# The delta-rule chain in full 128x128 matmuls, and three scale-and-bias products moved to ScalarE

## The chip, the cores and the metric

The kernel runs on one core of one Trainium2 chip. The metric is device time in microseconds of one execution. A core has five engines with a queue each, worked off in order: TensorE (PE in the profile), VectorE (DVE), ScalarE (ACT), GpSimd (POOL), and SyncE (SP), which issues the DMAs here. [...] TensorE writes PSUM; its weights are loaded by a separate instruction, shown as PEld.

## The reference

One decoder block on 512 rows of width 1024: an RMSNorm, a token mixer with two parallel branches (HGRN2 and RWKV-7) merged by sigmoid gates, and a gated convolutional FFN. The change touches both branches of the mixer. The RWKV-7 branch is this recurrence, for 16 heads of width 64:

```
def step(state, inp):                       # _rwkv7_scan
    r_t, w_t, k_t, v_t, a_t, b_t = inp
    sa = einsum('bhvk,bhk->bhv', state, a_t)
    state = state * w_t + sa[..., None] * b_t + v_t[..., None] * k_t
    y = einsum('bhvk,bhk->bhv', state, r_t)
    return state, y
```

The HGRN2 branch needs, per channel, `f = lb + (1 - lb) * sigmoid(hf)` and `k = 1 - f`, running products of `f` within half-chunks of 16 rows, and from these chunked attention scores. The RWKV key is `kr * (1 + (a - 1) * k_a)` with a constant `k_a` per channel.

## The kernel before

The program has two parts. The first, from about 55 us on, is the token mixer: for each of 66 blocks of 128 output columns a product of x with the input weights (`gemm`, L1144: 24 matmuls into the PSUM tile `zps`, or `vps` for the HGRN values; the operands are split into a high and a low fp32r half, so three matmuls for each of 8 pieces of the contraction), and beside it the two branches, for `hb` = 0 to 7 (128 channels, that is two RWKV heads). The second part, from about 743 us on, is the branch outputs, the mix and the FFN; nothing in it changes.

In the first part the order on every engine is not written out: generators (`front`, `solve`, `chain`, `hgrn`, `load`, `splits`, `evac`, `gemm`) yield operations, and `Plan` (L78 to L241) keeps a model time for each engine and issues the operation that can start first, with a rank and a bonus. `Plan.cost` holds the model's durations. The issue itself is L207, so that nearly all instructions of this part stand under that line; they are told apart by tiles.

For each `hb`, `front` (L702) makes from r, k, v and the decays the scaled operands of 8 chunks of 64 rows: `gt` (queries), `lr` (two masked 64x64 score blocks per chunk and head), `bkn` (keys, transposed). All three lie in one tile `X`. `solve` (L817) inverts the triangular blocks: `Q`. Then `chain` (L872) runs the 8 chunks one after the other; each is a step of the recurrence, with `h` the head, 0 or 1, on its own half of the partitions:

- z: `gt` times `sv` (state of one head above, values below), 128x64 weights, one matmul per head into halves of the tile `us`;
- y, first part: the same with the query columns of `gt`, into `yp`;
- `zs` is z copied out of PSUM by VectorE;
- u: `Q` times `zs`, 64x64 weights, one matmul per head;
- VectorE scales u by `rn2` into `sv`, one instruction per head;
- s: `bkn` times `sv`, 128x64 weights, one per head (not in the last chunk);
- y, second part: `lr` times `sv`, 64x64 weights, one per head, added to `yp` in PSUM;
- VectorE adds s to `sp`, the decayed state that ScalarE has made, for the next chunk's `sv`.

All these operands are fp32, and an fp32 matmul has two records in the profile (so x4 there is two matmuls). That makes 10 matmuls a step, in five pairs of which each covers half of TensorE's columns, or a quarter of its array, at a time. Behind the last step `chain` normalises y and stores it. `front` of `hb` waits for `chain` of `hb` - 2, whose `X` it takes; `chain` waits for `solve`; the `gemm` blocks fill the rest.

In `hgrn` (L966) VectorE makes the two halves of `f2` from `hf` by a scale and a bias (L972 to L975) and scans them into `p2`; GpSimd makes `hk` (L984), and in `front` the key factor `k2` (L736).

Of the kernel before, what the change touches and what calls it, by code (L numbers as in the profile page):

```python
# [16 lines left out]
P = 128  # L17
# [60 lines left out]
class Plan:  # L78
# [73 lines left out]
    def cost(self, op):  # L152
# [92 lines left out]
def block_kernel(ctx: ExitStack, tc: tile.TileContext, out: bass.AP, xT: bass.AP, xN: bass.AP,  # L245
# [146 lines left out]
    sgx = [pers.tile([P, NCH, 65], F32, name=f"sgx{i}") for i in range(2)]  # L392
# [3 lines left out]
    f2 = pers.tile([P, 2, 16, 17], F32, name="f2")  # L396
# [4 lines left out]
    for t_ in sgx:  # L401
        Gi.memset(t_[:, :, 0:1], 0.0)
    Gi.memset(f2[:, :, :, 0:1], 0.0)
# [256 lines left out]

    zwah = pers.tile([P, S], F32R, name="zwah")
# [40 lines left out]
    def front(hb):  # L702
# [13 lines left out]
        sg = sgx[hb % 2]  # L716
# [19 lines left out]
        yield G1.tensor_scalar(k2, ta, hka[:, hb : hb + 1], oka[:, hb : hb + 1], op0=ALU.mult, op1=ALU.add)  # L736
# [16 lines left out]
        lr = X[:, 4 * S : 6 * S].rearrange("p (n x c) -> p n x c", n=NCH, x=2)  # L753
        bkn = X[:, 6 * S : 8 * S].rearrange("p (n c) -> p n c", n=NCH)
# [17 lines left out]
        for h in range(2):  # L772
            q, o = hs[h], hs[1 - h]
            for half in range(2):
# [6 lines left out]
                yield V1.tensor_tensor(lr[q, n0 : n0 + 4, h], sc[q, :, h], mr[q, n0 : n0 + 4], op=ALU.mult)  # L781
                yield V1.tensor_tensor(lr[q, n0 : n0 + 4, 1 - h], sc[q, :, 1 - h],
# [10 lines left out]
        for h in range(2):  # L793
            for b in range(4):
                p0 = 64 * h + 16 * b
                yield D1.dma_start(lb_d[:, h, b].rearrange("n s t -> s n t"),
                                   lr[p0 : p0 + 16, :, h, 16 * b : 16 * b + 16])
        st_[hb] = [vt[hb], gt, lr, bkn, pel, rn2]
        fin.add(("lb", hb))
        plan.spawn("solve", solve(hb, lb_d, lr))  # L800
# [9 lines left out]
        for half in range(2):  # L810
            tp = pf.tile([P, 4, P], F32, name="tp", tag="f")
            for n in range(4):
                yield T1.transpose(tp[:, n], bks[:, 4 * half + n], ident)
            yield A1.copy(bkn[:, 4 * half : 4 * half + 4], tp)
        fin.add(("front", hb))

    def solve(hb, lb_d, lr):  # L817
# [16 lines left out]
        Q = mx.tile([P, NCH, 64], F32, name="Q", bufs=2)  # L834
# [5 lines left out]
        for n in range(NCH):  # L840
            for h in range(2):
                yield T1.matmul(fps[hs[h], n], lr[hs[h], n, h], Tn[hs[h], n], start=True, stop=True)
        fm = mx.tile([P, NCH, 64], F32, name="fm")
# [5 lines left out]
        yield V1.tensor_tensor(Q, Q, dps, op=ALU.add)  # L849
        yield V1.transpose(Tn.rearrange("p n c -> p (n c)"), Q.rearrange("p n c -> p (n c)"))  # L850
        fps2 = pf.tile([P, NCH, 32], F32, name="fps2", tag="s", bufs=1)
        fm2 = fm[:, :, 0:32]
        for h in range(2):
            a, b = slice(64 * h, 64 * h + 32), slice(64 * h + 32, 64 * h + 64)
            for n in range(NCH):
                yield T1.matmul(fps2[b, n], lr[a, n, h, 32:64], Tn[a, n, 0:32], start=True, stop=True)
# [8 lines left out]
        for h in range(2):  # L865
            a = slice(64 * h, 64 * h + 32)
            yield A1.copy(Q[a, :, 32:64], dps2[a])
        yield done(("front", hb))
        st_[hb].append(Q)
        fin.add(("solve", hb))  # L870

    def chain(hb):  # L872
        v, gt, lr, bkn, pel, rn2, bo, Q = st_.pop(hb)
        sv = mx.tile([P, NCH, 2, 64], F32, name="sv")
        vp = pus.tile([P, NT, P], F32, name="vp", tag="us")
# [48 lines left out]
        ys = mx.tile([P, NCH, 64], F32, name="ys")  # L924
        ym = small.tile([P, NCH], F32, name="ym")
        yield V1.tensor_reduce(ym, yp, axis=AX.X, op=ALU.add)
        yield V1.tensor_single_scalar(ym, ym, 1.0 / 64, op=ALU.mult)
        yield V1.tensor_tensor(ys, yp, ym.unsqueeze(2).broadcast_to([P, NCH, 64]), op=ALU.subtract)
        yield A1.activation(yp, ys, AF.Square)
        yss = small.tile([P, NCH], F32, name="yss")  # L930
        yield V1.tensor_reduce(yss, yp, axis=AX.X, op=ALU.add)
# [34 lines left out]
    def hgrn(hb):  # L966
        hf = hf_[hb]

        def c32(ap):
            return ap.rearrange("p (n c) -> p n c", n=16)  # L970

        yield V1.tensor_scalar(f2[:, 0, :, 1:17], c32(hf)[:, :, 15::-1], fb[:, hb : hb + 1], fa[:, hb : hb + 1],  # L972
                               op0=ALU.mult, op1=ALU.add)
        yield V1.tensor_scalar(f2[:, 1, :, 1:17], c32(hf)[:, :, 16:32], fb[:, hb : hb + 1], fa[:, hb : hb + 1],
                               op0=ALU.mult, op1=ALU.add)  # L975
        p2 = mx.tile([P, 2, 16, 17], F32, name="p2")
        yield V1.tensor_tensor_scan(p2.rearrange("p a n c -> p (a n c)"), f2.rearrange("p a n c -> p (a n c)"),
# [6 lines left out]
        yield G1.tensor_scalar(hk, hf, nfb[:, hb : hb + 1], fb[:, hb : hb + 1], op0=ALU.mult, op1=ALU.add)  # L984
# [57 lines left out]
        qs = mx.tile([P, 16, 32], F32, name="qs")  # L1042
        yield V1.tensor_tensor(qs, qi[:, 0:16], cq.rearrange("p t j -> p (t j)").unsqueeze(2).broadcast_to([P, 16, 32]),
# [473 lines left out]
```

## Time and profile before

| | us |
|---|---|
| time, median of 3 runs | 1256.02 (1255.92 to 1258.85) |
| profiled execution | 1255.5 |
| its span, first to last instruction | 1253.8 |
| busy in the span: PE, DVE, ACT, POOL | 1210.6, 732.7, 463.6, 536.0 |
| the second part's first matmul (`yps`) | 743.5 |

A start in the timeline is when an instruction begins; matmuls are pipelined, so the distance from one start to the next is what a matmul costs TensorE, and the duration beside it, which runs over the next ones, is not. The profile writes the weights' size of a matmul as 128\*64 (rows times columns), behind it the shape that it writes.

### The profile page before, as it was taken

The numbers are of one execution on the slowest core, as the hardware profiler recorded it, in microseconds if no ns is written. First come the engines' busy times: TensorE is split into PE (matmuls) and PEld (weight loads), VectorE is DVE, ScalarE is ACT, GpSimd is POOL, SyncE is SP. The second block draws the span as 40 slices with busy tenths as digits, with TensorE's granted clock in tenths as the row PEclk, the third lists the DMA queues.
The fourth block names the chain that finished last, engine by engine and source line by source line (L and its number), as shares of the span: only waits on it lengthen the run. The fifth ranks groups of instructions, "written<-read, shape, count | busy, mean of one in ns | idle before, by whom it ended". The sixth has DMA issues, their size and how long they took to land.

```text
span 1253.8 us, 19765 instructions
## 1 busy us (share of the span) xinstructions
PE 1210.6 (97%) x7748; PEld 949.7 (76%) x7748; DVE 732.7 (58%) x1563; ACT 463.6 (37%) x825; POOL 536.0 (43%) x420
## 2 busy tenths in 40 slices
PE   8889999999999999999999999999999999999997
PEld 6667668667668677686767888888988888888886
DVE  6988887787888988886746304335523232322213
ACT  5533334333343443343332532225534343342321
POOL 6444224342332423242424454432466575565631
PEclk9889899999999999999999999999999999999999
DMA  5121212112112122121221733254323232232332
GB/s 178 50 68 58 65 43 87 49 55 68 50 61 64 54 65 68 43 75 55 70 72 49 240 118 118 86 186 156 130 85 115 90 112 84 84 101 80 122 101 84
DMA packets 54061, 111.01 MB, mean 89 GB/s; under 512 B 21584, under 2 KB 24784, under 8 KB 53968
## 3 DMA queue, kind: packets, MB, share of 16 engines
q1 hardware_dynamic: 53968, 109.75, 27.6%
q8 instruction: 61, 1.00, 0.3%
q14 instruction: 32, 0.26, 0.1%
HBM read 100.29 MB, written 9.44 MB: 88 GB/s over the span
## 4 chain that ended last, share of the span: by engine, by line
PE 75%; DVE 15%; issue 3%; ACT 3%; POOL 2%; DMA 1%; SPq 0%; DVEq 0%; POOLq 0%; ACTq 0%
PE zps L207 20%; PE zps L323 6%; PE zps L322 6%; PE zps L321 6%; PE dn L321 3%; PE dn L323 3%; PE dn L322 3%; PE us L207 3%; PE sc L207 2%; PE yps L321 2%; PE yps L323 2%; PE yps L322 2%; PE vps L207 2%; PE mix L207 2%; DVE X L207 2%
## 5 line engine op out<-in xcount | busy, mean ns | idle before, releaser
L207 POOL TENSOR_TENSOR wlo_t<-raw,whi_t 128x512 fp32r<-128x512 f32 x134 | 184.6, 1397 | 351.3 <-ACT whi_t L207 319.8
L279 POOL TENSOR_TENSOR wlo_t<-raw,whi_t 128x1024 fp32r<-128x1024 f32 x80 | 194.6, 2439 | 96.4 <-ACT whi_t L279 96.2
L207 PE MATMUL zps<-xl,whi_t 128*128 128x512 f32 x488 | 201.3, 413 | 0.0
L207 PE MATMUL zps<-xh,wlo_t 128*128 128x512 f32 x488 | 201.2, 412 | 0.0
L207 PE MATMUL zps<-xh,whi_t 128*128 128x512 f32 x488 | 200.6, 411 | 0.0
L279 ACT CAST whi_t<-raw 128x1024 fp32r<-128x1024 f32 x80 | 83.3, 1049 | 175.5 <-DMA raw<-wup 64.5
L1378 DVE SCALAR_TENSOR_TENSOR u<-zps,pr,u 128x511 f32<-128x511 f32 x40 | 30.0, 750 | 190.7 <-ACT u L1377 190.7
L207 ACT CAST whi_t<-raw 128x1024 fp32r<-128x1024 f32 x71 | 74.4, 1048 | 147.1 <-PE zps L207 68.1
L321 PE MATMUL zps<-x2h,whi_t 128*128 128x512 f32 x320 | 125.5, 392 | 0.0
L323 PE MATMUL zps<-x2h,wlo_t 128*128 128x512 f32 x320 | 125.5, 392 | 0.0
L322 PE MATMUL zps<-x2l,whi_t 128*128 128x512 f32 x320 | 125.5, 392 | 0.0
L207 PEld LDWEIGHTS zps<-xl,whi_t 128*128 128x128 f32 x488 | 92.5, 190 | 20.6 <-issue 0.5
L207 PEld LDWEIGHTS zps<-xh,wlo_t 128*128 128x128 f32 x488 | 92.7, 190 | 20.1 <-issue 0.2
L207 PEld LDWEIGHTS zps<-xh,whi_t 128*128 128x128 f32 x488 | 92.8, 190 | 19.4 <-issue 0.2
L321 PEld LDWEIGHTS zps<-x2h,whi_t 128*128 128x128 f32 x320 | 60.2, 188 | 13.5
L322 PEld LDWEIGHTS zps<-x2l,whi_t 128*128 128x128 f32 x320 | 60.2, 188 | 13.5
L323 PEld LDWEIGHTS zps<-x2h,wlo_t 128*128 128x128 f32 x320 | 60.1, 188 | 13.4
L1403 POOL TENSOR_TENSOR th<-th,u 128x512 f32<-128x512 f32 x22 | 28.4, 1292 | 71.2 <-DVE u L1379 71.2
L207 ACT ACTIVATE sp<-sv,pel 64x64 f32<-64x64 f32 x96 | 33.0, 344 | 67.0 <-DVE sv L207 65.8
L207 PEld LDWEIGHTS us<-sv,X 128*64 128x64 f32 (+1 forms) x480 | 23.8, 134 | 39.7 <-issue 11.6
L207 DVE TENSOR_SCALAR sv<-us,rn 64x64 f32<-64x64 f32 x128 | 35.8, 280 | 29.0 <-PE us L207 25.3
L321 PE MATMUL yps<-oh,whi_t 128*128 128x512 f32 x128 | 50.2, 392 | 0.0
(375 smaller groups left out, 2601.0 us busy)
## 6 DMA issues: line engine op xcount, KB each, us to landing
raw<-win SPq DMA_DIRECT2D x64, 512.0 KB, 3.7
raw<-wup SPq DMA_DIRECT2D x44, 512.0 KB, 3.5
raw<-wdn SPq DMA_DIRECT2D x22, 512.0 KB, 3.5
raw<-wbr SPq DMA_DIRECT2D x16, 512.0 KB, 3.4
raw<-whi SPq DMA_DIRECT2D x8, 512.0 KB, 3.5
raw<-wout SPq DMA_DIRECT2D x8, 512.0 KB, 3.5
xt<-xT SPq DMA_DIRECT2D x8, 256.0 KB, 6.4
oa_d<-hg SPq DMA_DIRECT2D x8, 256.0 KB, 2.2
```

What stands on the lines that cost most here:

```text
L207: op.ins_ = self.seq(op.key, op.fn(*op.args, **op.kw))
L279: return A.copy(hi, raw), eng.tensor_tensor(lo, raw, hi.bitcast(F32), op=ALU.subtract)
L321: T.matmul(o, lh, rh, start=start, stop=False)
L322: T.matmul(o, lh, rl, start=False, stop=False)
L323: T.matmul(o, ll, rh, start=False, stop=stop)
L1378: V.scalar_tensor_tensor(u[:, 1:S], ps[:, 0 : S - 1], pc("cw1", b), u[:, 1:S], op0=ALU.mult, op1=ALU.add)
L1403: G.tensor_tensor(th, th, uv_, op=ALU.mult)
```

## The change

In `chain`, each pair becomes one or two matmuls over the whole array. z and the first part of y are one matmul per head, with all 128 columns of `gt`. `Q` is put into `qd`, a 128x128 block-diagonal tile per chunk (zeros elsewhere, set once by GpSimd for its two buffers), so u is one matmul for both heads. `lr` and `bkn` become `w2`, 128x128 per chunk and head, so s and the second part of y are one matmul per head; the block of `lr` that only `solve` needs is overwritten with zeros at the end of `solve`. Five matmuls a step stand where ten did, each with 128x128 weights and a moving operand of 64 columns, also in the first and last step.

The two parts of y now come out of different matmuls, and ScalarE copies them, per step and head, into `ys` and `yb`; VectorE adds these once per `hb`. The copy of z and the scaling of u are divided: VectorE takes head 0, ScalarE head 1. The results of a step take five of 16 slots in two PSUM banks. `f2` is gone: ScalarE writes `p2`, and the scan works in place; `hk` and `k2` also go to ScalarE. `sgx`, `Q`, `fm`, `qs` lose a buffer or share one. `Plan.cost` gets one more line.

```
+            elif n == 64 and m == 128:
+                op.us = 0.112
...
-        yield G1.tensor_scalar(k2, ta, hka[:, hb : hb + 1], oka[:, hb : hb + 1], op0=ALU.mult, op1=ALU.add)
+        yield A1.activation(k2, ta, AF.Identity, scale=hka[:, hb : hb + 1], bias=oka[:, hb : hb + 1])
...
-        lr = X[:, 4 * S : 6 * S].rearrange("p (n x c) -> p n x c", n=NCH, x=2)
-        bkn = X[:, 6 * S : 8 * S].rearrange("p (n c) -> p n c", n=NCH)
+        w2 = X[:, 4 * S : 8 * S].rearrange("p (n h c) -> p n h c", n=NCH, h=2)
...
+        qd = qds[hb % 2]
+        if hb < 2:
+            yield G1.memset(qd, 0.0)
...
+        for h in range(2):
+            yield A1.copy(qd[hs[h], :, hs[h]], Q[hs[h]])
...
+        for h in range(2):
+            yield G1.memset(w2[hs[h], :, 1 - h, hs[h]], 0.0)
         yield done(("front", hb))
...
+        for h in range(2):
+            yield G1.memset(sv[hs[h], 0, h], 0.0)
...
         for n in range(NCH):
-            for h in (1, 0):
-                yield T1.matmul(us[hs[h], zslot], gt[kp, n, h, h], sv[kp, n, h], start=True, stop=True)
-            for h in (1, 0):
-                yield T1.matmul(yp[hs[1 - h], n], gt[kp, n, h, 1 - h], sv[kp, n, h], start=True, stop=False,
-                                skip_group_check=True)
+            for h in range(2):
+                yield T1.matmul(zy[h], gt[:, n, h].rearrange("p x c -> p (x c)"), sv[:, n, h], start=True, stop=True)
             zs = small.tile([P, 64], F32, name="zs")
-            yield V1.tensor_copy(zs, us[:, zslot])
+            yield V1.tensor_copy(zs[hs[0]], zy[0][hs[0]])
+            yield A1.copy(zs[hs[1]], zy[1][hs[1]])
...
-            for h in (1, 0):
-                yield T1.matmul(us[hs[h], uslot], Q[hs[h], n], zs[hs[h]], start=True, stop=True)
             for h in range(2):
-                q = hs[h]
-                yield V1.tensor_scalar(sv[q, n, h], us[q, uslot], rn2[q, n : n + 1], None, op0=ALU.mult)
-            if n < NCH - 1:
-                for h in (1, 0):
-                    yield T1.matmul(us[hs[h], sslot], bkn[:, n, hs[h]], sv[:, n, h], start=True, stop=True)
-            for h in (1, 0):
-                yield T1.matmul(yp[hs[1 - h], n], lr[hs[h], n, 1 - h], sv[hs[h], n, h], start=False, stop=True,
-                                skip_group_check=True)
+                yield A1.copy(ys[hs[1 - h], n], zy[h][hs[1 - h]])
+            yield T1.matmul(us, qd[:, n], zs, start=True, stop=True)
+            yield V1.tensor_scalar(sv[hs[0], n, 0], us[hs[0]], rn2[hs[0], n : n + 1], None, op0=ALU.mult)
+            yield A1.activation(sv[hs[1], n, 1], us[hs[1]], AF.Identity, scale=rn2[hs[1], n : n + 1])
+            for h in range(2):
+                yield T1.matmul(sy[h], w2[:, n, h], sv[:, n, h], start=True, stop=True)
...
+            for h in range(2):
+                yield A1.copy(yb[hs[1 - h], n], sy[h][hs[1 - h]])
...
+        yield V1.tensor_tensor(ys, ys, yb, op=ALU.add)
...
-        yield V1.tensor_scalar(f2[:, 0, :, 1:17], c32(hf)[:, :, 15::-1], fb[:, hb : hb + 1], fa[:, hb : hb + 1],
-                               op0=ALU.mult, op1=ALU.add)
+        yield A1.activation(p2[:, 0, :, 1:17], c32(hf)[:, :, 15::-1], AF.Identity, scale=fb[:, hb : hb + 1],
+                            bias=fa[:, hb : hb + 1])
...
-        yield G1.tensor_scalar(hk, hf, nfb[:, hb : hb + 1], fb[:, hb : hb + 1], op0=ALU.mult, op1=ALU.add)
+        yield A1.activation(hk, hf, AF.Identity, scale=nfb[:, hb : hb + 1], bias=fb[:, hb : hb + 1])
```

What stands in a row on TensorE, before, in the fourth step of `hb` = 1 (the first `us` row and the `yp` row are z and the first part of y, the last row is u; shapes are those written, `X` holds `gt`, `lr` and `bkn`, and `bps` belongs to the bonus term):

```order
L207 MATMUL bps<-rkh,blk1r 128x512
L207 MATMUL bps<-rkl,blk1r 128x512
L207 MATMUL us<-sv,X_1205 64x64 x2
L207 MATMUL yp<-sv,X_1205 64x64 x2
L207 MATMUL zps<-xh,whi_t 128x512
L207 MATMUL zps<-xl,whi_t 128x512
L207 MATMUL zps<-xh,wlo_t 128x512
...
L207 MATMUL us<-zs,Q 64x64 x2
```

And in the changed kernel, in a step of `hb` = 1 (first u, then, past `aps` of the next block and four `zps`, s with the second part of y, one matmul per head, in slots of the tiles `us` and `yp`):

```order
L209 MATMUL us<-zs,qd_517 128x64
L209 MATMUL aps<-zwah,lw 128x512
L209 MATMUL aps<-zas,lw 128x512
L209 MATMUL zps<-xh,wlo_t 128x512
L209 MATMUL zps<-xh,whi_t 128x512
L209 MATMUL zps<-xl,whi_t 128x512
...
L209 MATMUL us<-sv,X_1203 128x64
L209 MATMUL yp<-sv,X_1203 128x64
```

What moved: no row of the chain is 64x64 on either axis of the array any more, and each stands singly or in twos between the wide rows. Counted along the whole of the first part on TensorE, a row that uses part of the array follows one that uses all of it in 240 places before and in 114 now; the number of runs of the other part-array matmuls (`sc`, `hsc`, `fps`, `dps`) is 110 before and 107 now.

On ScalarE, before, in a step of `hb` = 2, the chain has only the two decayed states `sp` (the other rows are the split of the next weights, an evacuation of `zps`, and the copy of transposed keys):

```order
L207 CAST whi_t<-raw 128x1024
L207 ACTIVATE r<-zps,cm 128x512
L207 ACTIVATE sp<-sv,pel 64x64 x2
L207 COPY X_2628<-tp 128x512
```

In the changed kernel, a whole step of `hb` = 2 on ScalarE:

```order
L209 COPY zs<-yp 64x64
L209 ACTIVATE sp<-sv,pel 64x64 x2
L209 COPY ys<-yp 64x64 x2
L209 CAST whi_t<-raw 128x1024
L209 ACTIVATE sv<-yp,rn_1804 64x64
L209 ACTIVATE hq<-zps 128x512
L209 ACTIVATE sgx<-wps,hw_128 128x8x64
L209 COPY yb<-yp 64x64 x2
```

What moved: half of z's copy and half of u's scaling now stand in this queue, with the states, the y copies and, here, a weight split between them.

More of the change, by code (lines that the diff above doesn't have):

```diff
@@ L391, in block_kernel @@
     Gi.memset(mh, 1.0)
-    sgx = [pers.tile([P, NCH, 65], F32, name=f"sgx{i}") for i in range(2)]
+    sgx = pers.tile([P, NCH, 65], F32, name="sgx")
     m65 = pers.tile([P, NCH, 65], F32, name="m65")
@@ L400, in block_kernel @@
     scm = pers.tile([P, NT, P], F32, name="scm")
-    for t_ in sgx:
-        Gi.memset(t_[:, :, 0:1], 0.0)
-    Gi.memset(f2[:, :, :, 0:1], 0.0)
+    Gi.memset(sgx[:, :, 0:1], 0.0)
     Gi.memset(scm, 0.0)
@@ L659, in c8 @@
         return ap.rearrange("p (n c) -> p n c", n=NCH)
+    qds = [mx.tile([P, NCH, P], F32, name=f"qd{i}") for i in range(2)]
     zwah = pers.tile([P, S], F32R, name="zwah")
@@ L715, in front @@
         yield T1.matmul(wps, lw[:, 0:P], zws, start=False, stop=True)
[L716 removed]
+        sg = sgx
         yield A1.activation(sg[:, :, 1:65], c8(wps), AF.Tanh, scale=0.5, bias=hw0[:, hb : hb + 1])
@@ L796, in front @@
                 yield D1.dma_start(lb_d[:, h, b].rearrange("n s t -> s n t"),
-                                   lr[p0 : p0 + 16, :, h, 16 * b : 16 * b + 16])
-        st_[hb] = [vt[hb], gt, lr, bkn, pel, rn2]
+                                   w2[p0 : p0 + 16, :, 1 - h, p0 : p0 + 16])
+        st_[hb] = [vt[hb], gt, w2, pel, rn2]
         fin.add(("lb", hb))
-        plan.spawn("solve", solve(hb, lb_d, lr))
+        plan.spawn("solve", solve(hb, lb_d, w2))
         bks = bk.rearrange("p n x c -> p n (x c)")
@@ L813, in front, with solve @@
                 yield T1.transpose(tp[:, n], bks[:, 4 * half + n], ident)
-            yield A1.copy(bkn[:, 4 * half : 4 * half + 4], tp)
+            dst = w2[:, 4 * half : 4 * half + 4].rearrange("p n h c -> p n (h c)")
+            dst = bass.AP(dst.tensor, dst.offset, [list(dst.ap[0]), [2 * P, 4], [P + 64, 2], [1, 64]])
+            yield A1.copy(dst, tp.rearrange("p n (h c) -> p n h c", h=2))
         fin.add(("front", hb))
-    def solve(hb, lb_d, lr):
+    def solve(hb, lb_d, w2):
         if hb > 0:
@@ L841, in solve @@
             for h in range(2):
-                yield T1.matmul(fps[hs[h], n], lr[hs[h], n, h], Tn[hs[h], n], start=True, stop=True)
-        fm = mx.tile([P, NCH, 64], F32, name="fm")
+                yield T1.matmul(fps[hs[h], n], w2[hs[h], n, 1 - h, hs[h]], Tn[hs[h], n], start=True, stop=True)
+        fm = Tn
         yield V1.tensor_tensor(fm, fps, mf.unsqueeze(1).broadcast_to([P, NCH, 64]), op=ALU.mult)
@@ L855, in solve @@
             for n in range(NCH):
-                yield T1.matmul(fps2[b, n], lr[a, n, h, 32:64], Tn[a, n, 0:32], start=True, stop=True)
+                yield T1.matmul(fps2[b, n], w2[a, n, 1 - h, b], Tn[a, n, 0:32], start=True, stop=True)
         for h in range(2):
@@ L923, in chain @@
         yield D1.dma_start(lgr, wlg[hb, :, 2 * P : 3 * P])
[L924 removed]
+        yield V1.tensor_tensor(ys, ys, yb, op=ALU.add)
         ym = small.tile([P, NCH], F32, name="ym")
[L926 removed]
+        yield V1.tensor_reduce(ym, ys, axis=AX.X, op=ALU.add)
         yield V1.tensor_single_scalar(ym, ym, 1.0 / 64, op=ALU.mult)
[L928 to L929 removed]
+        yield V1.tensor_tensor(ys, ys, ym.unsqueeze(2).broadcast_to([P, NCH, 64]), op=ALU.subtract)
+        yield A1.activation(yb, ys, AF.Square)
         yss = small.tile([P, NCH], F32, name="yss")
[L931 removed]
+        yield V1.tensor_reduce(yss, yb, axis=AX.X, op=ALU.add)
         yield from rsq1(yss, NCH, 64 * GN_EPS)
```

40 lines of the change are left out of this document (21 added, 19 removed).

## Prediction

> **What bounds the kernel now.** I read the page first: what each engine was busy for, and the chain of work that ended last.
>
> ```profile
> PE 1210.6 (97%) x7748; PEld 949.7 (76%) x7748; DVE 732.7 (58%) x1563; ACT 463.6 (37%) x825; POOL 536.0 (43%) x420
> PE 75%; DVE 15%; issue 3%; ACT 3%; POOL 2%; DMA 1%; SPq 0%; DVEq 0%; POOLq 0%; ACTq 0%
> ```
>
> TensorE carries three quarters of that chain. The change lies in the first part, so I cut that out by windows, and asked in its steady stretch, 140 to 620 us, what TensorE's matmuls waited for (waiter, releaser: us in total, times, longest).
>
> ```profile
> 55.00:700.00 645.00, 619.18 (x5060) 464.08 (x5060) 511.05 (x1278) 239.11 (x514) 224.83 (x198) 0.98 0.21 63
> PE us L207 <- DVE sv L207: 3.9, 6, 1.8
> ...
> PE sc L207 <- DVE sv L207: 0.2, 1, 0.2
> L207 ACT ACTIVATE sgGB<-zps x8: 585/588/592, 706.3 to 746.1; 128x512 f32<-128x512 f32 x8
> ```
>
> The eight rows of waits, of which these are the first and the last, add up to 14.4 us in 480: 3%. VectorE (third number of the window, 511 of 645) is the next engine, ScalarE (239) has room. The last row is the evacuation of the last eight weight blocks: these run on TensorE until 746 us, while the chain's last scaling (its row is below) is at 681. So the first part ends with TensorE's own list of work, and what TensorE no longer has to do before that comes off the end.
>
> **What a chain matmul costs TensorE** is in the timeline, by distances from start to start.
>
> ```profile
> 303.37 0.40 PE L207 MATMUL bps<-rkl,blk1r 128*128 128x512 f32 x1
> 303.70 0.34 PE L207 MATMUL us<-sv,X 128*64 128x64 f32 x4
> 303.86 0.29 PE L207 MATMUL yp<-sv,X 128*64 128x64 f32 x4
> 304.08 0.94 PE L207 MATMUL ups<-vn,k 128*128 128x128 f32 x6
> ...
> 305.09 0.40 PE L207 MATMUL zps<-xl,whi_t 128*128 128x512 f32 x1
> 305.41 0.33 PE L207 MATMUL us<-zs,Q 64*64 64x64 f32 x4
> 305.68 0.50 PE L207 MATMUL zps<-xh,wlo_t 128*128 128x512 f32 x1
> 306.01 0.40 PE L207 MATMUL zps<-xh,whi_t 128*128 128x512 f32 x1
> 306.24 0.40 PE L207 MATMUL zps<-xl,whi_t 128*128 128x512 f32 x1
> ...
> 307.18 0.40 PE L207 MATMUL zps<-xh,wlo_t 128*128 128x512 f32 x1
> 307.50 0.34 PE L207 MATMUL us<-sv,X 128*64 128x64 f32 x4
> 307.77 0.33 PE L207 MATMUL yp<-sv,X 64*64 64x64 f32 x4
> 308.03 0.51 PE L207 MATMUL zps<-xh,whi_t 128*128 128x512 f32 x1
> 308.37 0.60 PE L207 MATMUL tp<-ident,bk 128*128 128x128 f32 x4
> ```
>
> Undisturbed, a wide matmul takes 0.23 (306.01 to 306.24). Ahead of a matmul that uses part of the array it takes 0.32 or 0.33 (305.09 to 305.41), behind one 0.33 or 0.34 (305.68, 308.03): entering costs 0.10, leaving 0.105, together **0.205 a switch**. The pairs themselves: z 0.16, y behind it 0.22, together 0.38; u 0.27; s and y 0.27 and 0.26, together 0.53. Over 64 steps, of which 8 have no s: 64 x 0.38 + 64 x 0.27 + 56 x 0.53 + 8 x 0.26 = 73.4 us, without switches.
>
> Now the fp32 matmul over the whole array. Two places bound it, since none with 64 moving columns is in the trace: `ups` moves 128 columns, `nps` only 2.
>
> ```profile
> 614.84 0.39 PE L207 MATMUL zps<-xl,whi_t 128*128 128x512 f32 x1
> 615.07 0.83 PE L207 MATMUL ups<-vn,k 128*128 128x128 f32 x6
> 615.65 0.48 PE L207 MATMUL zps<-xh,wlo_t 128*128 128x512 f32 x1
> 615.97 0.40 PE L207 MATMUL zps<-xh,whi_t 128*128 128x512 f32 x1
> 398.00 0.95 PE L207 MATMUL nps<-blk,sq 128*128 128x2 f32 x8
> 398.80 0.36 PE L207 MATMUL vps<-whi_t,xl 128*128 128x256 f32 x1
> ```
>
> The wide one ahead of `ups` takes 0.23: no switch. From 615.07 to 615.97 three `ups` and a wide matmul take 0.90, so 0.67 / 3 = 0.22 each. Four `nps` take 0.80, 0.20 each, with a sixty-fourth of the moving columns: the price hangs on the 128 weight columns that each of the two records loads. So 64 columns cost between 0.20 and 0.22; I take **0.22**, and 320 of them (64 x 5) are 70.4 us.
>
> **TensorE's sum.** Chain matmuls 73.4 - 70.4 = 3.0 us less: halving their number alone is worth next to nothing. Switches: TensorE's order has 240 before and 114 after, 126 x 0.205 = 25.8 us less. The other part-array runs stay (110 and 107). Together **28.8 us**.
>
> [...]
>
> **What the other engines get.**
>
> ```profile
> L207 DVE TENSOR_SCALAR sv<-us,rn x128: 176/284/292, 157.0 to 680.7; 64x64 f32<-64x64 f32 x128
> L207 DVE TENSOR_SCALAR f<-hf,fb,fa 128x256 f32<-128x256 f32 x16 | 13.6, 868 | 2.2 <-ACT hf L207 2.0
> L207 DVE TENSOR_TENSOR ys<-ys,yss 128x512 f32<-128x512 f32 x8 | 7.0, 872 | 4.3 <-POOL yss L207 4.3
> L207 ACT ACTIVATE sp<-sv,pel 64x64 f32<-64x64 f32 x96 | 33.0, 344 | 67.0 <-DVE sv L207 65.8
> L207 ACT COPY sv<-vp 64x256 f32<-64x256 f32 x32 | 11.7, 367 | 8.3 <-PE vp L207 7.7
> L207 ACT COPY X<-tp 128x512 f32<-128x512 f32 x16 | 9.3, 584 | 28.6 <-PE tp L207 28.5
> L207 ACT ACTIVATE ta<-aps,ha 128x512 f32<-128x512 f32 x8 | 5.5, 684 | 7.8 <-PE aps L207 7.8
> L207 POOL TENSOR_SCALAR hk<-hf,nfb,fb 128x512 f32<-128x512 f32 x8 | 8.6, 1069 | 0.0
> L356 POOL MEMSET scm<- 128x512 f32 x1 | 0.5, 525 | 0.0
> L207 ACT CAST whi_t<-raw 128x1024 fp32r<-128x1024 f32 x71 | 74.4, 1048 | 147.1 <-PE zps L207 68.1 <-issue 57.5 <-DMA raw<-wup 7.8
> ```
>
> VectorE loses 64 scalings of 0.28 (17.9 us) and `f2` (13.6), and gains eight additions of 0.87 (7.0): 24.5 us less of 511. I count this as nothing, since TensorE seldom waits for it; shorter, its share stays at 80% of a shorter part. GpSimd gives up two products per `hb` (`hk`: 1.07 each) for small memsets (0.5 for 512 elements); it was busy 35% and nobody's release changes by more than that: nothing.
>
> ScalarE gains 320 copies of 64x64 from PSUM. The trace has none so small: between 0.15 (the two copies' line carried back to no elements: 0.367 less 256 times the slope, (0.584 - 0.367) / 256 = 0.85 ns) and 0.367, the 64x256 one. By that slope 64 elements take 0.20, which I take: 64 us. Further 64 scalings of 0.344 (22), 32 products of 0.5 to 0.7 like `ta` (19) and 16 copies into `qd` of 0.58 (9): 114 us, 239 becomes 353 of some 617: 57%. There is room on average, and the wide matmuls hide it as long as they stand between the links; what it costs where they don't is the rival below. I take 0 to 15 us and, by the cover below, nearest to 0.
>
> A new wait: half of zs, and half of the scaled u, come from ScalarE. Queued behind them are that engine's weight splits (1.05 each), for which GpSimd and then the gemm wait, and the copies of y, for which only the freeing of a slot waits. In the step shown for `hb` = 2 ScalarE has, from zs to the end of the scaling, 0.20 + 2 x 0.344 + 2 x 0.20 + 1.05 + 0.344 = 2.7 us. TensorE's cover from z to s is u (0.22) and, on average, 1.3 us of other matmuls on each side of it: 2.8 us. So a step with a split just fits, one without has a microsecond to spare.
>
> **Sum.** The profiled execution took 1255.5 us, 0.5 below the median. 1255.5 - 28.8 = 1226.7; I forecast **1227**.
>
> **Rivals.** (a) *ScalarE eats a part.* Six weight splits fall within each chain's eight steps; if half lie between zs and the scaling and cost 0.5 us uncovered, 24 x 0.5 = 12 us go back: 1239. For it: the cover is 0.1 us in such a step. Against: only 3% of waits now, with a VectorE that is far fuller. 0.17. (b) *ScalarE becomes the chain's bound: slower.* Place: zs and scaling in ScalarE's queue. Price: beyond 28.8 / 64 = 0.45 us of uncovered wait a step it decides; if each step met one split too many in the middle, 1.05 less the spare 0.4 = 0.65, 42 us come back: 1268. Against: splits are six for eight steps, not one each. 0.09. (c) *Half price.* The line added to the planner puts the new matmul at 0.112. Then 320 x 0.108 = 34.6 us more come off: 1192. Against: `nps`, 0.20 with two columns. 0.07. (d) *It doesn't do what it says:* the 0.10 on both sides belongs to the fp32 matmul of 64 columns or to the wait on `sv`, not to the part of the array. Then 126 switches stay, 3.0 us come off: 1252.5, which a measurement cannot tell from no change. Against: `ups`, also fp32, and entered at 0.23. 0.07.
>
> **Chances and range.** The forecast, 1215 to 1237, has 0.60. Range 1207 to 1247: it leaves out (b), (c) and (d), some 0.2, and holds (a) with ScalarE's 15 us and, below, VectorE's 24.5 us if a part of them does count. This kernel's measurements tell no change from one of 0.3%, 3.8 us: forecast, (a) and (c) are faster, 0.84; (d) the same, 0.07; (b) slower, 0.09.
>
> **What would show it.** Right: `zps` ahead of and behind the chain's rows at 0.23 and near it; u alone between wide matmuls 0.22 apart from its neighbours' 0.23; the last `sgGB` at about 717 us; ScalarE busy near 350 in the first part. Wrong: u at 0.11 (c); 0.33 beside full-size rows (d); waits of `us` for ACT `sv` or ACT `zs` above 15 us together (a), above 29 (b); a last `sgGB` that hasn't moved.

## The result, and the profile after

| | before | after |
|---|---|---|
| time, median us | 1256.41 (1255.92 to 1258.85, 4 runs) | 1300.95 (1300.05 to 1302.32, 4 runs) |
| span, profiled execution | 1253.8 | 1300.6 |
| last `sgGB` evacuation starts | 746.1 | 793.1 |

The ratio is 1.035, 95% interval 1.033 to 1.037: slower, where faster was forecast. From the pages: TensorE's granted clock in 40 slices of the span (tenths of full speed), first before; then, all after, busy times, clock, the chain that ended last, and the last evacuations of the first part:

```profile
PEclk9889899999999999999999999999999999999999
...
PE 1235.4 (95%) x7140; PEld 999.3 (77%) x7140; DVE 717.4 (55%) x1491; ACT 575.5 (44%) x1257; POOL 532.5 (41%) x444
PEclk9889998999999989769699999999999999999999
PE 72%; DVE 15%; ACT 6%; issue 4%; POOL 2%; DMA 1%; SPq 0%; DVEq 0%; POOLq 0%; ACTq 0%
L209 ACT ACTIVATE sgGB<-zps x8: 583/590/597, 753.8 to 793.1; 128x512 f32<-128x512 f32 x8
```

TensorE is still the bound and has 608 records fewer, yet the first part is 47 us longer; the second part has not changed. The clock row after has 7, 6 and 6 where all slices before have 8 or 9. The windows of the first part, before and then after (length, busy time of PE, PEld, DVE, ACT, POOL, the granted clock, DMA share, GB/s):

```profile
55.00:746.10 691.10, 665.28 (x5258) 501.20 (x5258) 520.76 (x1286) 260.43 (x538) 247.74 (x214) 0.99 0.23 71
```

```profile
55.00:793.10 738.10, 691.67 (x4657) 552.52 (x4657) 504.83 (x1214) 372.14 (x970) 244.70 (x241) 0.93 0.23 67
```

TensorE is idle for 691.10 - 665.28 = 25.8 us before and 46.4 after: 20.6 us more. Its busy time times its clock, summed over windows of 1 us, is 657.3 before and 645.0 after: by this measure the work itself did become less, by 12.3 us. What is left of the busy time, 8.0 and 46.7, is lost to a lower clock: 38.7 more. **-12.3 + 20.6 + 38.7 = +47.0.** So there are two questions: why TensorE waits, and why its clock falls.

**The price of a matmul is not among them.** The rows after that answer to the ones on which the price rested:

```profile
300.95 0.40 PE L209 MATMUL zps<-xh,whi_t 128*128 128x512 f32 x1
301.19 0.40 PE L209 MATMUL zps<-xl,whi_t 128*128 128x512 f32 x1
301.43 0.49 PE L209 MATMUL kps<-ident,kj 128*128 128x128 f32 x3
301.75 0.33 PE L209 MATMUL us<-zs,qd 128*128 128x64 f32 x2
301.89 0.48 PE L209 MATMUL zps<-xh,wlo_t 128*128 128x512 f32 x1
302.21 0.39 PE L209 MATMUL zps<-xh,whi_t 128*128 128x512 f32 x1
```

From u's start to the second wide row it is 302.21 - 301.75 = 0.46. A wide row alone takes 0.23 or 0.24 here, so 0.23 is left for u, and nothing for a switch. It is so over the whole first part where nothing waits at full clock: a wide row, one chain matmul and the next wide row take 0.69 together (median of 31 places), where a wide row, a pair of 64-column matmuls and the next took 0.925 before (41 places). (The last shape in a matmul's row, 128x64 here, is its moving operand; the text ahead of the prediction wrongly calls it what the matmul writes.)

**The waits.** Waiter, releaser, us in total, times, longest; on ScalarE from 140 to 660 us, on TensorE's weight loads from 140 to 700:

```profile
ACT yb L209 <- DVE sv L209: 56.8, 42, 3.2
ACT zs L209 <- DVE zs L209: 51.5, 39, 3.1
ACT sv L209 <- DVE sv L209: 32.7, 38, 2.0
```

```profile
PEld us L209 <- ACT ys L209: 16.9, 21, 2.0
PEld yp L209 <- ACT ys L209: 9.2, 12, 1.9
PEld yp L209 <- ACT yb L209: 8.6, 14, 1.8
PEld us L209 <- ACT sv L209: 7.3, 10, 1.2
...
PEld us L209 <- ACT zs L209: 1.0, 2, 0.7
```

ScalarE's half of zs reads nothing that VectorE's half writes, and still waits for it 39 times; and TensorE waits for `ys`, ScalarE's copies of y, which no matmul of the step reads. In the timeline:

```profile
307.44 0.70 ACT L209 ACTIVATE sp<-sv,pel 64x64 f32<-64x64 f32 x2
...
308.05 0.41 ACT L209 COPY ys<-us 64x64 f32<-64x64 f32 x2
...
308.51 0.30 PEld L209 LDWEIGHTS us<-zs,qd 128*128 128x128 f32 x2 [0.63 <-ACT ys L209]
308.51 0.43 PE L209 MATMUL us<-zs,qd 128*128 128x64 f32 x2 [0.19 <-ACT ys L209]
```

What these have in common is the PSUM bank: z of both heads and u lie in the tile `us` here, and the copies into `ys` read from it. So, by these waits, the program makes one engine wait for another when both touch one bank, and what the change divided between two engines runs in turn. Kernel 7 below bears this out: with the two heads' z in different banks the row ACT zs <- DVE zs is gone, and ScalarE's half waits for TensorE's z alone (`ACT zs L209 <- PE yp L209: 38.4, 40, 3.4`). zs's halves lie in different partitions, 64 each, and the waits above show them in turn all the same: 39 times, 51.5 us.

**The clock.** At fine resolution it has two values in the traced executions of both kernels, 1.00 and 0.50. In the changed kernel every fall and rise from 140 to 700 us lies on a grid of 3.413 us with one phase (all 16 edges within 0.02 us), so half clock comes in stretches of 3.41 us, each of which costs up to 1.71. There are 26, up to 44.4 us. Before, the last one ends at 140.7. Windows cut on that grid (from 458.91 to 486.22, some left out):

```profile
458.91:462.33 3.42, 3.42 (x28) 2.33 (x28) 2.71 (x7) 1.52 (x6) 0.00 (x0) 1.00 0.00 0
462.33:465.74 3.41, 3.41 (x36) 2.80 (x35) 0.66 (x3) 0.68 (x4) 0.00 (x0) 1.00 0.00 0
465.74:469.16 3.42, 3.42 (x30) 2.77 (x30) 2.60 (x8) 1.38 (x6) 0.00 (x0) 0.50 0.09 10
469.16:472.57 3.41, 3.41 (x12) 2.83 (x11) 0.09 (x1) 0.91 (x1) 2.42 (x2) 0.50 0.74 211
...
479.40:482.81 3.41, 1.91 (x15) 1.47 (x13) 3.31 (x10) 1.15 (x6) 1.46 (x2) 1.00 0.00 0
482.81:486.22 3.41, 3.30 (x19) 2.71 (x20) 2.09 (x11) 1.62 (x6) 0.90 (x2) 1.00 0.00 0
```

Behind 479.40, with 1.5 us of waits, the clock stays at 1.00, as it does behind three more windows with 1.5 to 1.7; behind 462.33, in which TensorE never waits, it falls. What ran in that one:

```profile
462.68 0.66 PE L209 MATMUL yp<-sv,X 128*128 128x64 f32 x4
463.27 0.70 PE L209 MATMUL hsc<-qi,kj 128*32 128x32 f32 x12
463.90 0.93 PE L209 MATMUL sc<-X,bk 64*128 64x128 f32 x6
464.76 0.43 PE L209 MATMUL yp<-sv,X 128*128 128x64 f32 x2
465.03 0.39 PE L209 MATMUL us<-sv,X 128*128 128x64 f32 x2
465.35 0.48 PE L209 MATMUL sc<-X,bk 64*128 64x128 f32 x2
```

No wide row: 36 records that move 32 to 128 columns each, with the weight loads busy for 2.80 of the 3.41 us. That suggested that the clock goes by the columns moved, not by how busy TensorE is; whatever lowers it is called the gate below.

### The profile page after: what moved, and what is told of

Same layout as the page of the kernel before. It is cut to its first block, busy times and chain, and to the rows that moved or that the text cites. A ratio compares the mean times of both kernels' runs of the same rounds, so it can differ in the third digit from the quotient of the medians.

```text
span 1300.6 us, 19101 instructions
## 1 busy us (share of the span) xinstructions
PE 1235.4 (95%) x7140; PEld 999.3 (77%) x7140; DVE 717.4 (55%) x1491; ACT 575.5 (44%) x1257; POOL 532.5 (41%) x444
## 4 chain that ended last, share of the span: by engine, by line
PE 72%; DVE 15%; ACT 6%; issue 4%; POOL 2%; DMA 1%; SPq 0%; DVEq 0%; POOLq 0%; ACTq 0%
PE zps L209 17%; PE zps L323 6%; PE zps L325 6%; PE zps L324 6%; PE us L209 4%; PE dn L325 3%; PE dn L323 3%; PE dn L324 3%; PE mix L209 3%; PE sc L209 3%; PE yp L209 2%; PE vps L209 2%; PE yps L323 2%; PE yps L325 2%; PE yps L324 2%
## 5 line engine op out<-in xcount | busy, mean ns | idle before, releaser
L209 POOL TENSOR_TENSOR wlo_t<-raw,whi_t 128x512 fp32r<-128x512 f32 x134 | 184.9, 1399 | 335.2 <-ACT whi_t L209 294.2
L209 PE MATMUL zps<-xh,whi_t 128*128 128x512 f32 x488 | 204.9, 420 | 0.0
L209 PE MATMUL zps<-xh,wlo_t 128*128 128x512 f32 x488 | 204.0, 418 | 0.8 <-POOL wlo_t L209 0.8
L209 PE MATMUL zps<-xl,whi_t 128*128 128x512 f32 x488 | 202.7, 415 | 0.0
L209 PEld LDWEIGHTS zps<-xh,wlo_t 128*128 128x128 f32 x488 | 95.2, 195 | 19.4 <-POOL wlo_t L209 1.5
L209 PEld LDWEIGHTS zps<-xl,whi_t 128*128 128x128 f32 x488 | 95.1, 195 | 18.1 <-issue 0.5
L209 PEld LDWEIGHTS zps<-xh,whi_t 128*128 128x128 f32 x488 | 95.3, 195 | 17.8
L209 ACT CAST whi_t<-raw 128x1024 fp32r<-128x1024 f32 x71 | 74.3, 1047 | 55.9 <-PE zps L209 29.2
L209 PEld LDWEIGHTS us<-sv,X 128*128 128x128 f32 x288 | 45.3, 204 | 18.7 <-ACT sv L209 7.7
L1414 POOL TENSOR_TENSOR th<-th,u 128x512 f32<-128x512 f32 x22 | 28.5, 1294 | 71.4 <-DVE u L1390 71.4
L209 PE MATMUL us<-sv,X 128*128 128x64 f32 x288 | 51.0, 289 | 5.1 <-ACT sv L209 4.1
L325 PE MATMUL yps<-oh,wlo_t 128*128 128x512 f32 x128 | 50.2, 392 | 0.0
```

The source lines that it names most:

```text
L209: op.ins_ = self.seq(op.key, op.fn(*op.args, **op.kw))
L325: T.matmul(o, ll, rh, start=False, stop=stop)
L1414: G.tensor_tensor(th, th, uv_, op=ALU.mult)
```

## The experiments

All times are medians; a ratio is to the kernel before on the same chip. A half-clock stretch is one of 3.41 us between 140 us and the end of the first part; idle is TensorE's, from 55 us to the last `sgGB`. The theories: **A**, work on one bank runs in turn, TensorE waits, the clock follows; **B**, ScalarE has too much to do; **C**, later **G**, the clock falls because the array is little in use; **W**, it falls because TensorE waits; **P** and **M**, the planner `Plan` spoils the order, since it knows nothing of banks (P) or has a wrong price for a chain matmul (M). Kernels bear the number of their label; there is no 4.

**1 and 2. Each half of the change alone.** Products on ScalarE in the kernel before; then the change with the products back on VectorE and GpSimd. Of the first, `k2`; `hk` and the halves of `f2` likewise:

```
-yield G1.tensor_scalar(k2, ta, hka[:, hb : hb + 1], oka[:, hb : hb + 1], op0=ALU.mult, op1=ALU.add)
+yield A1.activation(k2, ta, AF.Identity, scale=hka[:, hb : hb + 1], bias=oka[:, hb : hb + 1])
...
```

> The kernel before with only f2, hk and k2 on ScalarE, the chain as it was. Theory A (the loss comes from the chain: its reads of a PSUM bank by two engines stand in sequence, and TensorE's writes behind them; TensorE's clock then falls): the products cost nothing or gain a little, 1250 to 1258. Theory B (ScalarE has too much work, wherever it comes from): these 37 us of ScalarE's 114 bring a third of the loss, 1268 to 1275. Theory C (the clock falls because the whole-array fp32 matmuls of 64 columns keep the array idle half their time): as before, 1254 to 1258.

Measured 1254.24, ratio 0.996 (0.995 to 0.998), idle 18.9, six half-clock stretches. B is out; A and C hold.

> The changed kernel with the three products back on VectorE and GpSimd. A: the loss stays, 1290 to 1310. B: a third of it goes, 1283 to 1288. C: as changed, 1295 to 1305, granted clock near 0.96.

Measured 1295.71, ratio 1.030 (1.028 to 1.031). The products cost nothing; the loss is the chain's. A and C both hold and are not told apart.

**3 and 5. Banks, and the links on VectorE.**

```
+zy = [ua[:, (2 * n + h) % 8] for h in range(2)]
+us, sy = ub[:, (3 * n) % 8], [ub[:, (3 * n + 1 + h) % 8] for h in range(2)]
```

> The changed kernel with z and y in one PSUM bank and u, s and the second y in the other, where they took slots of both in turn: u no longer shares a bank with the copies of z's and y's results. A: TensorE's waits of u for ACT ys (some 31 us of 600 together) go, and the clock comes back in part: 1255 to 1280. B: no change, 1295 to 1305. C: no change in clock or time, 1295 to 1305.

Measured 1283.59, ratio 1.019 (1.016 to 1.022), 22 stretches: outside all three ranges. The waits for `ys` did go, but TensorE's weight loads now wait in the tile `yp` for ACT sv (20.8 us) and ACT zs (12.3), and idle is still 42.3. In the next one both halves of zs and of the scaling are on VectorE as well:

> As e3, and VectorE makes both halves of zs and of the scaled u, so that no link of the chain goes through ScalarE, which only copies y out. A: the links no longer stand in sequence across two engines; TensorE's waits fall to those of the kernel before, the clock stays at 1.0 in the steady stretch, and the 29 us of TensorE's work come off: 1225 to 1250. B: ScalarE has 30 us less to do, 1290 to 1297. C: clock and time as changed, 1295 to 1305.

Measured 1292.67, ratio 1.028 (1.026 to 1.031), 22 stretches: A's number missed by far, since the waits moved once more (the loads wait for DVE sv, 16.2 us in `yp` and 6.1 in `us`; idle 49.0). B's range holds it, but not B: with less for ScalarE to do it is 9 us slower than kernel 3. Neither a lighter ScalarE nor the bank of z alone is the answer, and the clock stayed low (a mean of 0.957 to 0.963 in its four runs; 0.984 to 0.993 in the kernel before's).

**6. The same order, twice the columns.** Kernel 3 with each chain matmul moving its 64 columns twice, into a second slot that nobody reads. `real` plans the first operation and issues it with the operands behind it; `rep` repeats 64 columns. So the order of instructions on TensorE, VectorE and ScalarE is that of kernel 3, row by row.

```
-yield T1.matmul(us, qd[:, n], zs, start=True, stop=True)
+yield real(T1.matmul(us, qd[:, n], zs, start=True, stop=True), ur, qd[:, n], rep(zs))
...
```

> The order of instructions on every engine is that of the kernel with the banks split (e3_banks: 1283.6 us, 22 stretches of 3.41 us at half the clock after 140 us, which cost 37.5 us). Only the chain's five matmuls a step move 128 columns instead of 64 (the same 64 twice). Theory G (the clock is halved for 3.41 us after a stretch of 3.41 us in which the array was in use less than about a third of the time, where a matmul that mostly loads weights counts as little as a wait): the columns cost TensorE next to nothing (ups with 128 columns took 0.22 us, the chain's with 64 take 0.23), the array is in use for 0.1 us more per matmul, and at least half of the 22 stretches go: 1250 to 1268 us. Theory A (waits between DVE and ACT on one bank are the loss, the clock only follows PE's waits): waits and clock stay, 1280 to 1288. If moved columns are paid for, 320 x 0.1 = 32 us more: 1315.

Measured 1276.16, ratio 1.013 (1.011 to 1.016). The windows from 140 to 700 us of kernel 3, then of this one:

```profile
140.00:700.00 560.00, 526.78 (x3877) 428.73 (x3877) 413.25 (x1052) 303.41 (x859) 175.23 (x184) 0.93 0.20 57
```

```profile
140.00:700.00 560.00, 525.46 (x3935) 426.14 (x3936) 415.78 (x1059) 305.74 (x867) 178.85 (x187) 0.96 0.20 57
```

22 stretches became 13, with as much waiting. More work for TensorE (5.7 us by busy time times clock) made the kernel 7.4 us faster. That is G's sign, and A's "waits and clock stay" is out; the time is short of G's range because the columns were not free and 13 stretches stayed.

**7 to 9. Where the waits come from.** Head 0's results in one bank, head 1's and u in the other (7); the planner's `MARGIN` of 0.6 us at 1.2 (8); its price for a chain matmul at 0.23 (9).

```
+zy, us = [ua[:, (2 * n) % 8], ub[:, (3 * n) % 8]], ub[:, (3 * n + 1) % 8]
+sy = [ua[:, (2 * n + 1) % 8], ub[:, (3 * n + 2) % 8]]
...
-MARGIN = 0.6
+MARGIN = 1.2
...
-                op.us = 0.112
+                op.us = 0.23
```

> The results of head 0 lie in one PSUM bank, those of head 1 and u in the other, so VectorE's copy of z and ScalarE's no longer touch one bank. Theory A: zs on ACT no longer runs behind zs on DVE, PE's waits for ACT zs, sv, ys and yb (36 us of all waits in the changed kernel, 140 to 700 us) fall to 20 or less, 1265 to 1285 us. Theory G: the time follows the number of stretches at half the clock, 1.71 us each; fewer waits give fewer of them, 10 to 20 remain, and 1270 to 1290. Both fall if the waits stay above 30 us.

Measured 1265.86, ratio 1.006 (1.004 to 1.008); idle 34.7, 16 stretches. The time lies at the lower end of A's range; G's 10 to 20 stretches hold, its 1270 to 1290 us does not. The waits fell less than A said: for ACT ys 19.2 us of the weight loads' (26.1 in the changed kernel), for ACT yb 5.9 (13.2). The scaling's halves, which read one u in one bank, still run in turn: ACT sv <- DVE sv, 37.3.

> The changed kernel with the planner's reserve between a link of VectorE or ScalarE and the matmul that waits for it at 1.2 us instead of 0.6, so more wide matmuls stand between. Theory P (the planner does not know of the banks and places the chain's matmuls too early): PE's waits fall from 36 us below 15, the stretches at half the clock from 26 to under 12, 1250 to 1275 us. Theory G agrees in the clock if the waits fall. Rival: the chain becomes longer than the work that covers it, wide matmuls run out in places, and it is 1300 or more.

Measured 1323.97, ratio 1.052 (1.050 to 1.054); idle 64.9, 41 stretches, 28 of them in one piece from 597 to 693 us. P failed; the rival holds: from 600 to 650 us not one row of `zps` or `vps` starts.

> The changed kernel with the planner's price of a chain matmul at 0.23, as measured, instead of 0.112. Theory M (the wrong price spoils the order): waits and half-clock stretches fall by half, 1265 to 1280 us. Theory G and P: a dearer chain matmul makes the planner put fewer wide ones between the links, so nothing is gained: 1290 to 1310, by the number of half-clock stretches.

Measured 1271.67, ratio 1.011 (1.009 to 1.013); idle 38.9, seven stretches. M's range holds it, though idle fell by a sixth and not by half; by G and P nothing was to be gained.

**10 to 12. Together.** Head banks and the price (10); the order of kernel 7 with 128 columns (11); kernel 10 with ScalarE's order in a step changed (12):

```
+        yield A1.activation(sp[h][hs[h]], sv[hs[h], n, h], AF.Identity, scale=pel[hs[h], n : n + 1])
 for h in range(2):
     yield T1.matmul(zy[h], gt[:, n, h].rearrange("p x c -> p (x c)"), sv[:, n, h], start=True, stop=True)
...
 yield A1.copy(zs[hs[1]], zy[1][hs[1]])
-        yield A1.activation(sp[h][hs[h]], sv[hs[h], n, h], AF.Identity, scale=pel[hs[h], n : n + 1])
+yield A1.copy(ys[hs[0], n], zy[1][hs[0]])
-for h in range(2):
-    yield A1.copy(ys[hs[1 - h], n], zy[h][hs[1 - h]])
 yield T1.matmul(us, qd[:, n], zs, start=True, stop=True)
+yield A1.copy(ys[hs[1], n], zy[0][hs[1]])
```

> Head banks (1265.9 us alone; 16 half-clock stretches after 140 us, PE idle 34.7 us in the first part) and the price 0.23 (1271.7 alone, 7 stretches) together. Theory M (the price spoils the order) and theory A (waits by bank) are different causes, so they add: 10 stretches or fewer, 1240 to 1258 us. Rival, order by chance (each change of the order lands some 10 us up or down, and the price did only that): no better than the better of the two, 1262 to 1280.

Measured 1250.05, ratio 0.996 (0.993 to 0.999), idle 35.5, seven stretches: some 51 us off the changed kernel, where the two alone gave 35 and 29. They add in the main.

> The order of instructions of e7_head_banks on every engine (1265.9 us, 16 half-clock stretches after 140 us), with 128 moving columns in the chain's matmuls instead of 64. Theory G, as in e6_banks_128col, where 22 stretches became 13 and 5.7 us of TensorE's work were added: 16 become 10 or fewer, 10 us of clock against 6 of columns, 1257 to 1266 us. If use of the array has nothing to do with it, the stretches stay at 14 to 18 and the columns make it 1270 to 1275.

Measured 1267.21, ratio 1.006 (1.004 to 1.008): 16 stretches became 12, and the columns (5.0 us of work) took back what that gave. It is G's sign again, but both ranges were missed, and a difference of four stretches is not much more than one program shows by itself (last section).

> As e10_heads_cost, with ScalarE's order in a step changed: the decayed states ahead of z, behind z only the half of zs and the one copy of y in u's bank, the other copy behind u. Theory A: u waits for two ScalarE operations instead of five (u's waits for ACT ys were 24.6 us of PE and its loads in e7_head_banks); PE's idle time falls by 10 us against e10_heads_cost, and with it some stretches: 1230 to 1250 us. Rival: the decayed states now delay zs by up to 0.7 us, and it is as e10_heads_cost or up to 15 us slower.

Measured 1245.50 (1243.30 to 1246.38), **ratio 0.989 (0.988 to 0.991): faster than both kernels.** Its waits on TensorE's weight loads for ScalarE, and its last evacuation:

```profile
PEld us L209 <- ACT yb L209: 12.3, 21, 2.0
PEld yp L209 <- ACT ys L209: 6.1, 12, 1.5
PEld us L209 <- ACT ys L209: 1.1, 2, 0.9
...
L209 ACT ACTIVATE sgGB<-zps x8: 586/590/594, 698.2 to 737.1; 128x512 f32<-128x512 f32 x8
```

The wait for `ys` in the tile `yp`, where u lies in kernels 7, 10 and 12, is down from 23.3 us in kernel 10 to 6.1, while the one for `yb` rose from 9.6 to 12.3; three stretches are left. The time is in A's range, but idle fell by 4 us (35.5 to 31.4), not by the 10 that A named. Against before the first part is 9.0 us shorter: work 657.3 to 640.2, idle 25.8 to 31.4, clock the rest.

**13 and 17. The gate by itself.** In the kernel before, extra fp32 matmuls ahead of six blocks of the FFN, where TensorE otherwise runs wide matmuls at 1.00 (in each window of 2 us from 980 to 1006 us of kernel 17): whole array with `kind` columns, as here, or parts of it. Their operands lie ready, and the block's first matmul overwrites their results.

```
+        for i in range(num):
+            if isinstance(kind, int):
+                T.matmul(ps[:, 0:kind], pr[:, 0:P], pr[:, P : P + kind], start=True, stop=True)
+            else:
...
```

> The kernel before with 45 extra fp32 matmuls (or 45 pairs) ahead of each of six blocks of the FFN, where TensorE otherwise runs wide matmuls without a wait at a clock of 1.00. The extra ones have operands that lie ready, so TensorE does not wait in them; their results are overwritten. In order: whole array with 64, 32, 2 and 128 moving columns, then pairs of 64x64 weights, then pairs of 128x64 weights. At 0.22, 0.22, 0.20, 0.22, 0.27 and 0.16 us each they take some 58 us, so that the time without any half clock is about 1315. Theory G: the clock is halved by too little use of the array, without any wait: 32 and 2 columns (used about 0.05 and 0.003 of 0.2 us) drop to 0.50 for three to four stretches of 3.41 us, 128 columns stay at 1.00, 64 columns (0.1 of 0.22) stay or are on the edge, pairs of quarters (0.1 of 0.27 in half of the array) drop, pairs of halves stay; some 15 us more, 1325 to 1345. Theory W (the gate follows TensorE's waits): 1.00 in all six places, 1315.

Measured 1321.02 in one run. The windows of the first four groups, 64, 32, 2 and 128 columns:

```profile
962.69:972.65 9.96, 9.96 (x91) 9.96 (x90) 0.29 (x1) 2.51 (x3) 7.11 (x4) 1.00 0.37 116
1000.30:1013.70 13.40, 13.40 (x91) 13.40 (x90) 0.29 (x1) 3.56 (x4) 9.46 (x5) 0.73 0.35 113
1042.83:1057.66 14.83, 14.83 (x91) 14.83 (x90) 0.36 (x1) 2.51 (x3) 7.10 (x4) 0.66 0.20 71
1087.08:1097.05 9.97, 9.97 (x92) 9.97 (x90) 0.30 (x1) 3.35 (x4) 7.13 (x4) 1.00 0.32 106
```

TensorE is busy throughout. With 64 and 128 columns (9.96 / 45 = 0.22 us each, both) the clock stays; with 32 and 2 it falls, to 0.73 and 0.66 over the whole group. W is refuted, and G's main claim shown: the clock falls without any wait when matmuls move few columns. The time is below G's range, since the pairs took 5.4 us a group where 12 and 7 were reckoned. That is too short to tell anything of them, so:

> As e13_gate_probe (32 and 2 columns at half clock, 64 and 128 at 1.00, always without a wait), now whole array with 48 and with 40 columns (45 matmuls each, 10 us), then 120 pairs of 64x64 weights, 120 single ones of 64x64, 120 pairs of 128x64 and 120 single 128x64. Use by columns: 64 moved in 0.22 us stayed, 32 did not; so 48 is open and 40 should drop. If the gate weighs the part of the array in use, the single quarters (a quarter of the array at most) drop and, nearer the edge, single halves and pairs of quarters stay or drop together; if it counts only that columns move, none of the four drops, since pairs take 0.12 us for 0.1 us of columns.

Measured 1347.46 in one run; whole array with 48 and 40 columns, pairs of quarters, single quarters:

```profile
963.09:976.16 13.07, 13.07 (x91) 13.06 (x90) 0.29 (x1) 2.61 (x3) 7.11 (x4) 0.75 0.29 104
1005.52:1019.92 14.40, 14.40 (x91) 14.40 (x90) 0.29 (x1) 3.56 (x4) 9.45 (x5) 0.68 0.33 110
1049.80:1063.94 14.14, 14.14 (x481) 14.07 (x481) 0.26 (x1) 2.51 (x3) 7.13 (x4) 1.00 0.24 78
1091.90:1106.04 14.14, 14.14 (x242) 14.07 (x241) 0.20 (x1) 3.56 (x4) 9.46 (x5) 1.00 0.35 114
```

With 48 and 40 columns it falls, to 0.50 in the windows of 2 us from 970 to 978 us and from 1012 to 1024. So the edge lies between 48 and 64 columns in 0.22 us. A single quarter of the array holds the clock as well as a pair (halves too, 1.00), so the part in use does not count as G's guess for the quarters had it. What fits all ten groups is the columns moved per time: 64 in 0.12 us and 64 or more in 0.22 hold, 48 or fewer in 0.22 do not. The third of the time, in G's line for kernel 6, the half that C has for kernel 1 and the 0.1 us that G counts for 64 moved columns were estimates of mine, and no run shows them; measured are 0.22 us a matmul for 128 columns and for 64 alike (9.97 and 9.96 / 45), and the edge between 48 and 64.

It does not fit every fall in the kernels. Ahead of the fall at 602.28 in the changed kernel TensorE waits for 0.08 us in all, and it runs mostly the 32x32 weights of `solve`, each moving 32 columns in some 0.07 us, more per time than 64 in 0.22:

```profile
598.69 1.01 PE L209 MATMUL fps<-Tn,X 32*32 32x32 f32 x30
599.63 1.16 PE L209 MATMUL sc<-X,bk 64*128 64x128 f32 x8
...
601.52 0.98 PE L209 MATMUL dps<-Q,Tn 32*32 32x32 f32 x27
```

The falls at 587.98 in kernel 3 and at 426.24 in kernel 13, there in the part that is the kernel before, follow the same rows. A sixteenth of the array may count for less than a quarter does; no run tests it.

**14 to 16. Chance or cause?** Two more prices in the changed kernel; and kernel 12 with the price left at 0.112.

> The changed kernel with the planner's price of a chain matmul at 0.17 (0.112: 1301, 0.23: 1271.7). Theory M (the price itself): between the two, 1278 to 1295. Chance (any change of the order moves the time by some 10 to 30 us either way): anywhere from 1265 to 1315, with no order among the four prices.

> The changed kernel with the price at 0.30, above what was measured (0.23). Theory M: no better than at 0.23, 1270 to 1290, since the planner now sees TensorE later than it is. Chance: anywhere from 1265 to 1315.

Measured 1293.60 (1290.86 and 1296.34) and 1287.91 (1287.59 and 1288.23): 0.112, 0.17, 0.23 and 0.30 give 1301, 1294, 1272 and 1288 (26, 17, 7 and 12 stretches), lowest at the measured price, as M has it. But chance's range holds both new times as well, so M stays likely, not shown: another order always brings chance with it.

> Head banks and the order of ScalarE of e12_heads_cost_order (1245.5) with the price left at 0.112 (head banks alone 1265.9, with the price 1250.1). Theory A: the order takes two to three ScalarE operations from ahead of u whatever the price, 1250 to 1262 us. If the order helps only by what it does to the plan, 1262 to 1275.

Measured 1253.87, ratio 0.997 (0.994 to 1.001), idle 25.4 (34.7 without the order), 14 stretches: A holds at the old price as well.

## Why the prediction was wrong, step by step

*TensorE is the bound.* Right, and misleading: a term for TensorE's work is only the end's term as long as waits and clock stay as they are. Both moved, by more than the work.

*Matmul prices and switches.* Right in kind: no switch beside the chain's rows, whole-array 0.23. Mis-sized in the sum: the step "320 of them are 70.4 us" took 0.22 where the row shows 0.23, 3 us; of the 28.8 us forecast, 12.3 came in the changed kernel, 17.1 in kernel 12 and 23.9 in kernel 16 (657.3 to 633.3). The switches did go: in the traces a part-array row follows a whole-array one 241 times before and 115 times after. Why kernels with the same matmuls differ in work was not traced.

*ScalarE's time and the new wait.* **This step failed:** "the copies of y, for which only the freeing of a slot waits", and with it "so a step with a split just fits". u's matmul waited for these copies, which stood ahead of it and in its bank (26.1 us for `ys`); ScalarE's halves waited for VectorE's (51.5 us for zs, 32.7 for the scaling), so the sum of ScalarE's own operations (2.7 us against a cover of 2.8) left out the largest part of the time. TensorE's idle time grew by 20.6 us. Banks (kernel 7, idle 34.7) and ScalarE's order (kernel 16) brought it to 25.4, where it was before. ScalarE's load was not the cause: it has 1257 operations in the changed kernel and in kernel 12, which is faster than the kernel before. The marker I had named, waits of `us` for ACT sv and zs above 15 us, would have missed it: the loads have 7.3 and 1.0; it was `ys` and `yb`.

*The price given to the planner.* I used the added line only as a rival's evidence on hardware ("half price"), and never asked what a planner does with a price of half the measured one. Kernel 9 puts some 29 us on it, kernel 10 another 16 on top of the banks; that 0.30 is worse than 0.23 speaks for the price itself, but the order's chance is in each of these, and it is not shown apart.

*The clock.* **The sum had no term for it, and it is the largest:** 38.7 us. It was 1.00 from 140 to 700 us before, and I carried that over. Kernel 13 shows that too few moved columns suffice (32 in 0.22 us, TensorE busy throughout), kernel 6 that they matter here (22 stretches to 13 in the same order). How it comes about in each place is argued, not shown: matmuls of 64 columns at 0.23 us among `sc` and `hsc` rows leave stretches with too few moved columns, and waits of a microsecond do the rest; ahead of three of the eight falls stand `solve`'s 32x32 rows, which the change leaves as they are. The two are not apart: of the eight falls in the changed kernel, six follow a stretch in which TensorE was idle for 0.6 to 1.5 us, two a stretch with next to no wait.

*VectorE and GpSimd as nothing, products as free.* Right for the products (kernel 1); the scalings taken from VectorE were not tested apart.

*Rivals.* (c) and (d) are out by the rows above: 0.23, and no switch where nothing waits. Of (b), the sign and place, ScalarE in the chain, were right; its mechanism, weight splits ahead of zs, is not what the waits show.

## What to carry to other kernels

When a change divides a step between engines, look up which PSUM bank each operation touches, and what stands in the new engine's queue ahead of the link: the two halves of zs had no data in common and still ran in turn (39 waits, 51.5 us). A price in a planner belongs to the change like an instruction, and is measured first. Where small matmuls stand between wide ones, look at the columns moved in every 3.41 us, the length of a half-clock stretch here, before and after a saving in small ones: in the changed kernel the clock took 38.7 us where the work gave 12.3.

## What the runs showed of the hardware

The clock changes on a grid of 3.413 us: all 16 edges from 140 to 700 us in the changed kernel and the eight from 45 to 141 us in the kernel before lie on one each, and in kernel 17 the two falls last 10.2 and 13.6 us by windows of 2 us, three and four times that. Counted from the first instruction the grid is at 0.70 us in the execution of the kernel before and at 1.53 in the changed kernel's. What lowers the clock need not be an idle TensorE: in kernel 17 it was busy all through and the clock dropped to 0.50 at 48 columns per 0.22 us; in kernel 13 it stayed at 1.00 at 64.

One program does not always meet the same number of half-clock stretches: ten runs of kernel 10 fell into two groups, six from 1248.89 to 1250.19 us at a mean clock of 0.986 to 0.990, four from 1257.37 to 1261.62 at 0.975 to 0.982. The kernels before, 13 and 17 show the same: the first part has the same rows in the same order in all three, and after 141 us it met none, two and three half-clock stretches in the executions traced. So a few stretches more or less, some microseconds, lie within one program.

Back to back, a pair of 64x64 weights takes 0.12 us and a single one as long (14.14 / 120 each, kernel 17; 128x64 likewise, 14.15 / 120); a whole-array matmul of 64 columns takes 0.22 (9.96 / 45, kernel 13). So among its like a pair costs about half of a whole-array matmul; the old chain's single pairs, 0.16 to 0.27 and a switch of 0.205, never saw that.
